# One more weight slot, shared row buffers and an earlier scatter in a two-layer mixture-of-experts trunk

## The chip, the cores and the metric

The kernel runs on one core of one Trainium2 chip. The metric is the device time of one launch in microseconds (us). Before the change it is 742.02 us, the median of three runs (740.44 to 742.1). The profiled execution, from which all rows below come, took 742.91 us; its span from the first to the last instruction is 740.9 us.

## The reference

256 tokens of 1024 features pass through two layers; everything is float32. Layer 1 is retention (four heads, chunks of 128) with a gated output, layer 2 is causal attention (eight heads; with 256 tokens there is a single block, so the selection of past blocks is empty). Each is followed by a mixture of experts:

```python
def hier_moe(x, w_rg, b_rg, w_re, b_re, w_gate, w_up, w_down):
    ...
    g_prob = softmax(t @ w_rg + b_rg)           # 4 groups, the best one
    e_logits = ...                              # 4 experts in it, the best two
    combine = group_w[:, :, None] * within[:, None, :]
    for g in range(G):
        hg = silu(t @ w_gate[g]) * (t @ w_up[g])
        y = y + (hg * combine[:, g, :, None]) @ w_down[g]
```

There are 16 experts per layer, each with a gate and an up matrix of 1024 x 512 and a down matrix of 512 x 1024. Each token uses two of them. All 16 experts' weights have to be read once per layer: 96 MB (in units of 1,048,576 bytes), beside 48 MB of dense weights in all. The layers end in a residual sum, the whole in a normalisation.

## The kernel before

**Weights as units in a ring.** All weights are cut beforehand into units of 1 MB (8 KB in each of 128 partitions). `Ring` holds a list of the units in the order of their use and a list of free slots in on-chip memory. `add` appends a unit; `issue` (L147) starts the transfer of the next unit as soon as a slot is free; `done` gives a slot back when the last matmul that reads it has been placed, and issues again. All these transfers stand in the queue of one engine, SyncE (SP), in the order of the list, each behind a wait for its slot. There are 20 slots that are always in the ring (19, and one that is free after retention), and in an expert stage some more: two or three `flex` buffers that the dense stages use otherwise, the buffer of `h` while its content stands in PSUM, and `N_EXTRA` slots of a pool `late` that is opened with the expert stage (none before the change). `ring.cap` lets an expert stage fetch at most `CAPX` = 2 units of what follows it.

**An expert layer** (`moe`, called twice). Its first part routes the tokens: logits, choice of the group and of two experts, and each token's place in its experts. Up to 64 tokens go to each expert. Two experts are worked on together as a pair `j` (0 to 7): their 2 x 64 token rows fill the 128 partitions of one buffer. The units of a pair are four of gate, four of up, four of down; each holds its part of both experts. `h`, the residual stream, is copied to PSUM (`total`, four banks) and to a table `rows` in memory off the chip. For the first pair the rows are gathered by matmuls; for all others GpSimd's indirect DMA fetches them (`pull`, L947) into `xn`.

**The loop over pairs** (L1226 on; TensorE's and ScalarE's instructions stand in the order of the program here, the other engines' are placed by the scheduler). For pair `j`:

1. `silu` of the gate product (L1204), the four up units by `grow(j, "u", ...)` (matmuls of `expand`, L982; one unit serves two of the eight steps `k`), then `gate` multiplies both (L1210).
2. `turn_in` (L953) transposes the rows `xn` of pair j+1 and evicts them to `xg`, half on VectorE (L940) and half on ScalarE (L944); `COLS` says which half goes where.
3. `turned` (L997) transposes the gated product of pair j; VectorE copies the first half of it to `hd` (L999), ScalarE the second (L1000).
4. `scatter` of the pair before, j-1 (L1029, L1030): eight matmuls that add its outputs to `total`; four for each half `n` of the features.
5. `slots(j + 2)` computes which tokens stand in pair j+2, and starts its `pull`.
6. `project` (L1010): the down projection with the four down units into two PSUM banks.
7. `parts` evicts these in two parts, `yh` on ScalarE (L1021) and `yl` on VectorE (L1022), into four buffers of 2 KB that serve this alone (tag `ys`).
8. `grow(j + 1, "g", ...)`: the gate units of the next pair.

In the last pair of a layer the scatter of the pair before stands between `turned` and `project` as well; then its own `parts` and `scatter` follow, and `finish` (the final normalisation) or `restore`. `more()` is a loop for experts with over 64 tokens; it does not run with these inputs.

The lines at which a pair's turning, scatter and projection follow one another are

```python
                    hd = turned(hh, work("hd").rearrange("p (k j) -> p k j", k=4))
                    if ahead:
                        scatter(*ahead)
                    if j + 2 < NP:
                        slots(j + 2, ps)
                    yp = project(both, hd, weight_of(j), done_of(j))
```

**Buffers that the change touches.** `flex(n, ...)` gives a buffer with a tag; a new tile under the same tag waits until the readers of the one before are done. `flex3` (8 KB) holds `xl`, the low part of the transposed stream in the dense stages, and then, in an expert stage, `held`: `xn` and `xg`, 4 KB each. `work` is a rotation of two buffers of 2 KB for `gl` (the silu output) and `hd`.

Of the kernel before, what the change touches and what calls it, by code (L numbers as in the profile page):

```python
# [37 lines left out]
COLS = 0, 1  # L38
# [157 lines left out]
def trunk(ctx, tc, x, x_t, dense_in, moe_in, gain_in, par_in, fin_in, rot_in, dec_in, con_in, out):  # L196
    nc = tc.nc
    V = nc.vector
    N_BASE, N_FLEX, N_EXTRA = 20, 2, 0
# [13 lines left out]

    def x_parts():
        return flex(2, [128, KD, T], F32R, "xh"), flex(3, [128, KD, T], F32R, "xl")
# [27 lines left out]
    def moe_units(layer):  # L243
        for j in range(NP):
            for n, name in enumerate("gud"):
                for u in range(4):
                    U["moe", layer, j, name, u] = ring.add(
                        moe_in[layer, j, 4 * n + u].rearrange("p (k n) -> p k n", k=2 if name == "d" else 4))
# [18 lines left out]
    ident_b = const.tile([128, 128], BF16, name="ident_b")  # L267
# [192 lines left out]
    def retention():  # L460
        with tc.tile_pool(name="ret_w", bufs=2, reuse_waits="tile") as wpool:
# [98 lines left out]
            for n, (a, b, unit, pieces) in enumerate(FIRST):  # L560
# [3 lines left out]
                if n == 0:  # L564
# [14 lines left out]
            nc.gpsimd.affine_select(out=ident_b, in_=ones_b, compare_op=OP.is_equal, fill=0.0, base=0,  # L579
                                    pattern=[[-1, 128]], channel_multiplier=1)  # L580
# [187 lines left out]
    def router(layer, junk):  # L768
# [3 lines left out]
        held = flex(3, [128, 2, D], F32, "held")  # L772
        xn = held[:, 0]
        xg = held[:, 1].rearrange("p (k j) -> p k j", k=KD)
# [28 lines left out]
    def moe(layer):  # L803
        g0 = G_FFN[layer]
        with tc.tile_pool(name="extra", bufs=1, side="right", reuse_waits="tile") as late, \
# [219 lines left out]
            def scatter(ys, st, end=False):  # L1025
                for n in range(2):
# [52 lines left out]
            def slots(j, bank=pt):  # L1079
                RS[j], idx = slot_values(sel_of(j), [cs[:, tt, j] for tt in range(NT)],  # L1080
                                         [con[:, C_SELC + 12 * n:C_SELC + 12 * n + 12] for n in range(2)], bank)
                if j:
                    pull(idx, xn)
# [128 lines left out]
            with tc.manual_schedule(engines={mybir.EngineType.PE}):  # L1212
# [9 lines left out]
                slots(1)  # L1222
                grow(0, "g", range(4, 8))
                ring.open([h.rearrange("p t d -> p (t d)")], moe_end[layer])
                ahead = None
            with tc.manual_schedule(engines={mybir.EngineType.PE, mybir.EngineType.Activation}):  # L1226
                for j in range(NP):
# [8 lines left out]
                    if j + 1 < NP:  # L1236
                        for n in range(2):
                            turn_in(xn, xg, range(4 * n, 4 * n + 4), COLS[n])
                    hd = turned(hh, work("hd").rearrange("p (k j) -> p k j", k=4))
                    if ahead:  # L1240
                        scatter(*ahead)
                    if j + 2 < NP:
                        slots(j + 2, ps)
                    yp = project(both, hd, weight_of(j), done_of(j))
                    st = transposed_select(rs, t1("ST", [128, T], F32R, bufs=2))
                    if j + 2 < NP:
                        ahead = parts(yp), st
                        grow(j + 1, "g", range(0, 8))
                    elif j + 1 < NP:
# [93 lines left out]
```

## Time and profile before

| | |
|---|---|
| median of three runs | 742.02 us (740.44 to 742.1) |
| profiled execution | 742.91 us, span 740.9 us |
| TensorE busy | 720.5 us (97%) |
| VectorE, ScalarE, GpSimd busy | 320.1, 270.4, 35.9 us |
| chain that ended last | TensorE 62%, DMA 34%, VectorE 2% |
| moved | 263.24 MB, 355 GB/s in the mean |
| granted clock of TensorE | 0.997 in the mean |

Times within the span are counted from its start. The stages are: retention up to about 204 us, routing and start of the first expert layer to about 217, its pairs to about 415, attention to about 521, routing again, and the pairs of the second expert layer and the end. A busy share is no measure of what limits a stage: a matmul counts as busy through its pipeline, so TensorE can look full while it waits a little for each unit. Rows of transfers give the issue on the sync queue; "landing" is when the data is reported as there.

### The profile page before, as it was taken

To read this page: it belongs to the slowest core of one execution; us is meant where nothing else is said; L and a number is where in the kernel's file an instruction comes from. 1 tells how busy PE (TensorE), PEld (TensorE's weight loads), DVE (VectorE), ACT (ScalarE), POOL (GpSimd) and SP (SyncE) were. 2 spreads that over 40 slices of the span, in tenths; PEclk is the share of its full clock that TensorE was granted. 3 is DMA by queue.
4 is the path that set the end of the run, shared out by engine and by line. 5 is a ranking of instruction groups with operands and counts; after the bars stand their busy time and mean duration, and the time that the engine had idled before them with its cause. 6 is when DMAs were issued, how large, how long until landed. Compare 5 with 4: busy or idle time off the path is not lost.

```text
span 740.9 us, 10093 instructions
## 1 busy us (share of the span) xinstructions
PE 720.5 (97%) x3652; PEld 430.1 (58%) x3652; DVE 320.1 (43%) x893; ACT 270.4 (36%) x550; POOL 35.9 (5%) x48
## 2 busy tenths in 40 slices
PE   8999999999999999999999999999999999999984
PEld 6988898887863434443343688888733344434431
DVE  4976688667661202211110677765721121112103
ACT  5667554667431111111110778674411111111112
POOL 0000000001000000000000003130010000000000
PEclk9999999999999999999999999999999999999998
DMA  8999646577879999999999799757899999999993
GB/s 246 421 420 420 228 145 243 207 278 274 323 283 388 422 419 419 419 423 419 419 421 404 315 422 421 290 211 303 318 397 421 420 421 418 423 419 421 420 410 122
DMA packets 43366, 263.24 MB, mean 355 GB/s; under 512 B 5695, under 2 KB 6975, under 8 KB 13616
## 3 DMA queue, kind: packets, MB, share of 16 engines
q1 hardware_dynamic: 40752, 256.85, 86.5%
q0 software_dynamic: 2560, 5.71, 2.1%
q8 instruction: 30, 0.49, 0.3%
q14 instruction: 24, 0.20, 0.1%
HBM read 263.12 MB, written 3.15 MB: 359 GB/s over the span
## 4 chain that ended last, share of the span: by engine, by line
PE 62%; DMA 34%; DVE 2%; issue 1%; SPq 0%; ACT 0%; DVEq 0%; POOLq 0%; ACTq 0%
DMA slot<-in_moe_dram 22%; PE ps L982 10%; PE acc L347 10%; PE acc L345 10%; PE acc L346 10%; DMA h<-in_moe_dram 8%; PE pt L1010 7%; DMA held<-rows,idx 2%; PE acc L383 2%; PE acc L381 2%; PE acc L382 2%; PE ps L794 1%; DMA slot<-in_dense_dram 1%; PE pt L953 1%; PE pt L884 1%; PE acc L1030 1%
## 5 line engine op out<-in xcount | busy, mean ns | idle before, releaser
L982 PE MATMUL ps<-slot,held 128*64 128x512 f32 x816 | 184.8, 594 | 2.0 <-DMA slot<-in_moe_dram 1.6
L982 PEld LDWEIGHTS ps<-slot,held 128*64 128x64 f32 x816 | 58.5, 137 | 116.7 <-issue 104.7
L341 DVE SCALAR_TENSOR_TENSOR wlo<-slot,gain,whi 128x512 fp32r<-128x512 f32 x144 | 107.0, 752 | 37.4 <-ACT whi L340 35.8
L340 ACT ACTIVATE whi<-slot,gain 128x512 fp32r<-128x512 f32 x144 | 102.9, 721 | 55.4 <-PE acc L346 37.0
L1210 DVE SCALAR_TENSOR_TENSOR gl<-ps,rs,gl 128x256 f32<-128x256 f32 x32 | 14.0, 480 | 194.5 <-PE ps L982 194.5
L1010 PE MATMUL pt<-slot,hd 128*64 128x512 f32 x416 | 96.2, 596 | 1.0 <-DVE idx L962 0.5
L345 PE MATMUL acc<-whi,xh 128*128 128x512 f32 x224 | 91.1, 407 | 0.6 <-ACT whi L340 0.6
L346 PE MATMUL acc<-whi,xl 128*128 128x512 f32 x224 | 87.6, 391 | 0.0
L347 PE MATMUL acc<-wlo,xh 128*128 128x512 f32 x224 | 87.5, 393 | 0.1
L1022 DVE TENSOR_TENSOR yl<-pt,yh 128x512 fp32r<-128x512 f32 x32 | 22.1, 691 | 99.9 <-ACT yh L1021 99.9
L1021 ACT ACTIVATE yh<-pt 128x512 fp32r<-128x512 f32 x32 | 19.1, 597 | 115.5 <-PE pt L1010 115.5
L1010 PEld LDWEIGHTS pt<-slot,hd 128*64 128x64 f32 x416 | 28.5, 137 | 53.1 <-issue 51.1
L944 ACT ACTIVATE held<-pt,gain 128x128 f32<-128x128 f32 x60 | 17.2, 368 | 102.5 <-PE pt L953 99.0
L1204 ACT ACTIVATE gl<-ps,rs 128x256 f32<-128x256 f32 x32 | 13.4, 470 | 106.3 <-PE ps L982 106.3
L347 PEld LDWEIGHTS acc<-wlo,xh 128*128 128x128 f32 x224 | 42.0, 188 | 10.0 <-DVE wlo L341 0.5
L345 PEld LDWEIGHTS acc<-whi,xh 128*128 128x128 f32 x224 | 42.2, 188 | 8.9 <-ACT whi L340 0.9
L346 PEld LDWEIGHTS acc<-whi,xl 128*128 128x128 f32 x224 | 42.2, 188 | 8.2
L338 DVE TENSOR_TENSOR wlo<-slot,whi 128x512 fp32r<-128x512 f32 x44 | 30.2, 689 | 21.0 <-ACT whi L337 18.2
L337 ACT ACTIVATE whi<-slot 128x512 fp32r<-128x512 f32 x44 | 27.8, 632 | 28.3 <-DVE wlo L338 16.3
L381 PE MATMUL acc<-xh,whi 128*128 128x256 f32 x128 | 35.9, 281 | 1.7 <-ACT whi L340 1.7
L383 PE MATMUL acc<-xh,wlo 128*128 128x256 f32 x128 | 36.2, 284 | 0.4 <-DVE wlo L341 0.3
L382 PE MATMUL acc<-xl,whi 128*128 128x256 f32 x128 | 35.6, 279 | 0.0
(226 smaller groups left out, 933.1 us busy)
## 6 DMA issues: line engine op xcount, KB each, us to landing
slot<-in_moe_dram SPq DMA_DIRECT2D x152, 1024.0 KB, 19.8
slot<-in_dense_dram SPq DMA_DIRECT2D x43, 1024.0 KB, 17.5
flex_slot<-in_moe_dram SPq DMA_DIRECT2D x22, 1024.0 KB, 19.8
slot_v<-in_moe_dram SPq DMA_DIRECT2D x8, 1024.0 KB, 19.6
h<-in_moe_dram SPq DMA_DIRECT2D x6, 1024.0 KB, 19.8
slot<-in_dense_dram SPq DMA_DIRECT2D x16, 256.0 KB, 6.4
rows<-h POOLq DMA_DIRECT2D x2, 1024.0 KB, 8.8
flex_slot<-in_moe_dram SPq DMA_DIRECT2D x4, 512.0 KB, 17.7
```

The costliest lines, as they stand in the source:

```text
L337: nc.scalar.activation(hi, w, AF.Copy)
L338: V.tensor_tensor(lo, w, hi.bitcast(F32), op=OP.subtract)
L340: nc.scalar.activation(hi, w, AF.Copy, scale=g)
L341: V.scalar_tensor_tensor(lo, w, g, hi.bitcast(F32), op0=OP.mult, op1=OP.subtract)
L345: nc.tensor.matmul(p, a, wh, start=start, stop=False)
L346: nc.tensor.matmul(p, l, wh, start=False, stop=False)
L347: nc.tensor.matmul(p, a, wl, start=False, stop=stop)
L381: nc.tensor.matmul(d, wh[:, s], xh[:, k], start=(k == 0 and c % 2 == 0), stop=False)
L382: nc.tensor.matmul(d, wh[:, s], xl[:, k], start=False, stop=False)
L383: nc.tensor.matmul(d, wl[:, s], xh[:, k], start=False, stop=(k == KD - 1 and c % 2 == 1))
L982: nc.tensor.matmul(p[s * w:(s + 1) * w], xg[:, k, s * w:(s + 1) * w], weight(name, k, s), start=(k == 0), stop=(k == KD - 1))
L1010: nc.tensor.matmul(yp[n][s * w:(s + 1) * w], hd[:, k, s * w:(s + 1) * w], weight("d", k, s)[:, n * 512:(n + 1) * 512], start=(k == 0), sto ...
```

## The change

It does the following:

- `N_EXTRA` is 1: an expert stage has one more slot of 8 KB per partition, in the pool `late`, open to the units of that stage only.
- The `ys` buffers are gone. The low half of the features (`n` = 0) of `yh` and `yl` goes to a tile `ylow` under the new tag `flex4`, 4 KB, the other half to the `work` rotation. `flex4` also holds `xn` (`rows_in`). `xl` is split into two tiles of 4 KB (`Halves`), in `flex3` and `flex4`; `xg` has `flex3` alone. `ST` has one buffer instead of two, and the unused `ident_b` is dropped.
- The order of the units: gate unit 0 of pair j+1 stands ahead of the four down units of pair j.
- In the loop the scatter of a pair follows its own projection, with gate step pair 0, 1 of the next pair between `turned` and `project` and steps 2, 3 between `parts` and `scatter`. The pull for pair j+2 follows the scatter, then gate steps 4 to 7. For pair 6 only the half `n` = 1 is scattered there; the half `n` = 0 follows the gating of pair 7, ahead of its `turned`.
- `COLS` swaps the engines of the two evictions in `turn_in`; the small product of `slots` goes to a `pt` bank instead of `ps`; `transposed_select` stands ahead of `project`.

```diff
-COLS = 0, 1
+COLS = 1, 0
...
-    N_BASE, N_FLEX, N_EXTRA = 20, 2, 0
+    N_BASE, N_FLEX, N_EXTRA = 20, 2, 1
...
     def x_parts():
-        return flex(2, [128, KD, T], F32R, "xh"), flex(3, [128, KD, T], F32R, "xl")
+        return flex(2, [128, KD, T], F32R, "xh"), Halves([flex(3 + n, [128, 4, T], F32R, f"xl{n}") for n in range(2)])
+
+    def rows_in():
+        return flex(4, [128, D], F32, "xn")
...
+            for n in range(3):
+                if n == 2 and j + 1 < NP:
+                    add(j + 1, 0, 0)
                 for u in range(4):
+                    if j == 0 or n + u:
+                        add(j, n, u)
...
             def parts(yp):
                 ys = []
+                low = flex(4, [128, 2, 512], F32R, "ylow")
                 for n in range(2):
-                    ys.append([t1(name, [128, 512], F32R, bufs=4, tag="ys") for name in ("yh", "yl")])
+                    ys.append([work(name, F32R) if n else low[:, i] for i, name in enumerate(("yh", "yl"))])
...
                     if j + 1 < NP:
                         for n in range(2):
                             turn_in(xn, xg, range(4 * n, 4 * n + 4), COLS[n])
+                    else:
+                        scatter(ys, st, ns=(0,))
                     hd = turned(hh, work("hd").rearrange("p (k j) -> p k j", k=4))
-                    if ahead:
-                        scatter(*ahead)
+                    if j + 1 < NP:
+                        grow(j + 1, "g", range(0, 2))
                     if j + 2 < NP:
-                        slots(j + 2, ps)
+                        idx = slots(j + 2)
+                    st = transposed_select(rs, t1("ST", [128, T], F32R))
                     yp = project(both, hd, weight_of(j), done_of(j))
-                    st = transposed_select(rs, t1("ST", [128, T], F32R, bufs=2))
-                    if j + 2 < NP:
-                        ahead = parts(yp), st
-                        grow(j + 1, "g", range(0, 8))
-                    elif j + 1 < NP:
-                        ahead = parts(yp), st
-                        grow(j + 1, "g", range(0, 4))
+                    if j + 1 < NP:
+                        ys = parts(yp)
+                        grow(j + 1, "g", range(2, 4))
+                        scatter(ys, st, ns=range(0 if j + 2 < NP else 1, 2))
+                        if j + 2 < NP:
+                            xn = rows_in()
+                            pull(idx, xn)
+                            grow(j + 1, "g", range(4, 8))
+                            continue
                         with tc.issue_after(ring.last.ins):
                             more()
```

## Rows read from the trace of the kernel before

**Rows 1.** The page's 40 equal slices of the span (18.5 us each): the GB/s that were moved.

```profile
GB/s 246 421 420 420 228 145 243 207 278 274 323 283 388 422 419 419 419 423 419 419 421 404 315 422 421 290 211 303 318 397 421 420 421 418 423 419 421 420 410 122
```

**Rows 2.** The table by stage: stretch in us, its length, busy us of PE, PEld, DVE, ACT and POOL with their instructions, granted clock, DMA share, GB/s.

```profile
255.00:398.00 143.00, 142.63 (x691) 56.17 (x689) 25.25 (x90) 20.88 (x55) 5.00 (x5) 1.00 1.01 420
415.00:521.00 106.00, 105.34 (x511) 87.59 (x512) 74.22 (x170) 73.51 (x155) 15.28 (x17) 1.00 0.84 336
...
636.00:717.00 81.00, 79.75 (x386) 30.81 (x384) 12.34 (x40) 12.87 (x32) 1.99 (x2) 1.00 1.02 420
```

**Rows 3.** The chain that ended last, its last transfer: start, length, what.

```profile
697.02 19.80 DMA slot<-in_moe_dram
```

**Rows 4.** TensorE in order of time over one pair of the second expert layer: `turn_in` of one pair, the first gate units behind its projection, `turn_in` of the next pair.

```profile
595.94 1.09 PE L953 MATMUL pt<-ident,held 128*128 128x128 f32 x8
...
606.25 1.89 PE L982 MATMUL ps<-flex_slot,held 128*64 128x512 f32 x8
...
620.09 1.09 PE L953 MATMUL pt<-ident,held 128*128 128x128 f32 x8
```

**Rows 5.** The same table as rows 2, microsecond by microsecond, at the start of the first and of the second expert layer; the last two columns are the DMA share and the GB/s.

```profile
213.00:214.00 1.00, 1.00 (x14) 1.00 (x11) 1.00 (x8) 0.00 (x0) 0.00 (x0) 1.00 0.83 311
214.00:215.00 1.00, 1.00 (x11) 0.88 (x12) 0.81 (x8) 0.63 (x2) 0.00 (x0) 1.00 0.14 57
215.00:216.00 1.00, 1.00 (x7) 0.42 (x8) 1.00 (x4) 0.00 (x0) 0.00 (x0) 1.00 0.08 33
216.00:217.00 1.00, 1.00 (x8) 0.29 (x4) 0.51 (x3) 0.00 (x0) 0.00 (x0) 1.00 1.06 205
...
533.00:534.00 1.00, 1.00 (x6) 0.29 (x4) 0.97 (x4) 0.00 (x0) 0.00 (x0) 1.00 0.86 360
534.00:535.00 1.00, 1.00 (x8) 0.39 (x6) 0.32 (x2) 0.00 (x0) 0.00 (x0) 1.00 0.90 221
535.00:536.00 1.00, 1.00 (x8) 0.19 (x4) 0.00 (x0) 0.00 (x0) 0.00 (x0) 1.00 0.63 221
```

**Rows 6.** The sync queue in order of time at the start of both expert layers.

```profile
204.61 0.33 SPq L147 DMA_DIRECT2D flex_slot<-in_moe_dram  x1
208.92 0.33 SPq L147 DMA_DIRECT2D slot<-in_moe_dram  x1
215.08 0.33 SPq L147 DMA_DIRECT2D h<-in_moe_dram  x1
...
527.07 0.78 SPq L147 DMA_DIRECT2D flex_slot<-in_moe_dram  x1
533.77 0.33 SPq L147 DMA_DIRECT2D h<-in_moe_dram  x1
```

**Rows 7.** In order of time, pair 0 of the first expert layer: the transposes of `turned`, the two copies to `hd`, the projection.

```profile
232.12 0.60 PE L997 MATMUL ps<-ident,gl 128*128 128x128 f32 x4
...
232.75 0.42 DVE L999 COPY hd<-ps 128x256 f32<-128x256 f32 x1 [0.18 <-PE ps L960]
...
233.23 3.22 PE L1010 MATMUL pt<-slot,hd 128*64 128x512 f32 x14 [0.48 <-DVE idx L962]
...
233.33 0.40 ACT L1000 ACTIVATE hd<-ps 128x256 f32<-128x256 f32 x1
```

**Rows 8.** In order of time, the last pair of each expert layer: in the second one the last up unit, gating, transposes, first scatter matmul, copy to `hd`, last scatter matmul, projection; of the first one the last up unit and the projection.

```profile
716.87 1.94 PE L982 MATMUL ps<-slot,held 128*64 128x512 f32 x8 [0.54 <-DMA slot<-in_moe_dram]
...
718.91 0.87 DVE L1210 SCALAR_TENSOR_TENSOR gl<-ps,rs,gl 128x256 f32<-128x256 f32 x2 [14.51 <-PE ps L982]
...
719.54 0.74 PE L997 MATMUL ps<-ident,gl 128*128 128x128 f32 x4 [0.73 <-DVE gl L1210]
...
720.03 0.49 PE L1029 MATMUL acc<-yh,ST 128*128 128x512 f32 x1
...
720.31 0.42 DVE L999 COPY hd<-ps 128x256 f32<-128x256 f32 x1 [0.53 <-PE ps L997]
...
721.74 0.40 PE L1030 MATMUL acc<-yl,ST 128*128 128x512 f32 x1
...
722.07 1.08 PE L1010 MATMUL pt<-slot,hd 128*64 128x512 f32 x4
...
398.41 1.94 PE L982 MATMUL ps<-slot,held 128*64 128x512 f32 x8 [0.54 <-DMA slot<-in_moe_dram]
...
403.59 1.08 PE L1010 MATMUL pt<-slot,hd 128*64 128x512 f32 x4
```

**Rows 9.** All gathers by GpSimd (L947): count, duration in ns (least, median, most), first and last start; time from issue to landing.

```profile
L947 POOL DMA_INDIRECT held<-rows,idx x14: 988/999/1136, 222.0 to 672.5; - x14
...
DMA to landing us min/median/max: 8.1/8.6/9.1
```

**Rows 10.** Two transfers of the last pair of the second layer, down unit 1 and the last piece of down unit 3: the issue, and the time from it to landing.

```profile
L147 SPq DMA_DIRECT2D flex_slot<-in_moe_dram x1: 328/328/328, 702.0 to 702.0; - x1
...
DMA to landing us min/median/max: 19.9/19.9/19.9
...
L147 SPq DMA_DIRECT2D slot<-in_moe_dram x1: 1819/1819/1819, 711.9 to 711.9; - x1
...
DMA to landing us min/median/max: 15.1/15.1/15.1
```

**Rows 11.** The page's list of transfers: out and in, queue, count, KB each, median us from issue to landing.

```profile
slot<-in_moe_dram SPq DMA_DIRECT2D x152, 1024.0 KB, 19.8
```

**Rows 12.** The table of rows 2 for the seven microseconds around the last up units.

```profile
713.00:720.00 7.00, 5.17 (x23) 1.34 (x20) 0.87 (x2) 0.00 (x0) 0.00 (x0) 1.00 1.00 406
```

More of the change, by code (lines that the diff above doesn't have):

```diff
@@ L212, in flex_slot, with __init__, __getitem__ @@
         return flex(n, [128, 2048], F32, f"flex_slot{n}")
+    class Halves:
+        def __init__(self, parts):
+            self.parts = parts
+        def __getitem__(self, at):
+            p, ks, *rest = at
+            if isinstance(ks, int):
+                return self.parts[ks // 4][(p, ks % 4, *rest)]
+            n = ks.start // 4
+            assert ks.stop <= 4 * n + 4
+            return self.parts[n][(p, slice(ks.start - 4 * n, ks.stop - 4 * n), *rest)]
     def x_parts():
-        return flex(2, [128, KD, T], F32R, "xh"), flex(3, [128, KD, T], F32R, "xl")
+        return flex(2, [128, KD, T], F32R, "xh"), Halves([flex(3 + n, [128, 4, T], F32R, f"xl{n}") for n in range(2)])
+    def rows_in():
+        return flex(4, [128, D], F32, "xn")
     def acc():
@@ L244, in moe_units, with add @@
         for j in range(NP):
-            for n, name in enumerate("gud"):
+            def add(j, n, u):
+                name = "gud"[n]
+                U["moe", layer, j, name, u] = ring.add(
+                    moe_in[layer, j, 4 * n + u].rearrange("p (k n) -> p k n", k=2 if name == "d" else 4))
+            for n in range(3):
+                if n == 2 and j + 1 < NP:
+                    add(j + 1, 0, 0)
                 for u in range(4):
-                    U["moe", layer, j, name, u] = ring.add(
-                        moe_in[layer, j, 4 * n + u].rearrange("p (k n) -> p k n", k=2 if name == "d" else 4))
+                    if j == 0 or n + u:
+                        add(j, n, u)
         for u in (2, 3):
@@ L1023, in parts, with scatter @@
                 return ys
-            def scatter(ys, st, end=False):
-                for n in range(2):
+            def scatter(ys, st, end=False, ns=range(2)):
+                for n in ns:
                     for tt in range(NT):
@@ L1081, in slots @@
                                          [con[:, C_SELC + 12 * n:C_SELC + 12 * n + 12] for n in range(2)], bank)
-                if j:
-                    pull(idx, xn)
+                return idx
             def weight_of(j):
@@ L1221, in moe @@
                 select(1, pos)
-                slots(1)
+                pull(slots(1), xn)
                 grow(0, "g", range(4, 8))
                 ring.open([h.rearrange("p t d -> p (t d)")], moe_end[layer])
-                ahead = None
             with tc.manual_schedule(engines={mybir.EngineType.PE, mybir.EngineType.Activation}):
```

8 lines of the change are left out of this document (2 added, 6 removed).

## The prediction

> **What bounds the kernel now.** I read the page's slices first: in the two expert stretches (the 14th to 22nd and the 30th to 39th slice) the moved bytes stand at 418 to 423 GB/s but for their first and last slices, while in the dense stretches they go up and down [rows 1]. The table by stage says the same: 255 to 398 us and 636 to 717 us run at 420 GB/s with a DMA share above 1.00, attention (415 to 521 us) at 336 GB/s with TensorE busy for 105.34 of 106 us [rows 2]. TensorE is also "busy" in the expert stretches, but the chain of waits settles who sets the end there: it runs back through weight transfers only, and the last one before the end is the 697.02 us issue that takes 19.80 us to land [rows 3]. A pair of experts is 12 units of 1 MB, 12 x 1.0486 MB / 420 GB/s = 30.0 us of transfer; TensorE needs 24.15 us for the same pair where nothing keeps it waiting (595.94 to 620.09 us) [rows 4]. So each expert layer ends at (sum of its bytes) / 420 GB/s, plus every microsecond in which the engines of the DMA stood still since the layer began, plus the tail behind the last up unit. Attention between them is bound by TensorE and passes a shift on whole.
>
> The stand-still is in the rows per microsecond: in layer 0 the rate falls to 311, 57, 33 and 205 GB/s from 213 to 217 us; in layer 1 to 360, 221 and 221 from 533 to 536 us [rows 5]. The sync queue shows why: it had no free slot. In layer 0 it issues at 204.61 and 208.92 us and then nothing until `h` comes free at 215.08; in layer 1 its last issue of the routing is at 527.07, and the next is `h` at 533.77 us [rows 6]. As shares of 420 GB/s the missing parts are 0.26 + 0.86 + 0.92 + 0.51 = 2.55 us and 0.14 + 0.47 + 0.47 = 1.08 us.
>
> **The change, part by part.** *One more unit slot.* It holds 1 MB, 2.50 us of transfer at 420 GB/s. It comes with the expert stage, beside flex slot 1, whose transfer goes out at 204.61 us [rows 6]; its bytes belonged to the dense stage's split weights, whose last reader is the same last dense matmul that frees that flex slot. So I expect its issue between 204.6 and 209.3 us, and 2.50 us more queued work: it fills the hole of 2.55 us in layer 0, gain 2.50. In layer 1 all that can be filled is the hole, 1.08 us: the rest of the megabyte only moves later what runs on without a stop (397 to 423 GB/s from there to the last slices [rows 1]). Bounds: 0 in both layers if the slot is released only after the hole; 2.50 in both if smaller dips later on vanish too. I take 2.5 + 1.1 = 3.6 us, since the holes are the rows nearest to it.
>
> *Order of units and gate steps.* Gate unit 0 of the next pair is fetched and used ahead of the four down units. It is the same 12 MB per pair, and behind the last up unit come the same four down units as before. TensorE's matmuls are the same too. Between the turning and the down projection the old kernel has eight scatter matmuls to cover the eviction of `hd`; now one gate unit, 13.84 us / 8 = 1.73 us [rows 4], covers it. Cost 0 while the transfers are behind; without that cover it would be at most the 0.42 us copy plus 0.40 us on ScalarE per pair [rows 7], and TensorE has 30.0 - 24.15 = 5.8 us to spare per pair. The swapped eviction order, one `ST` buffer instead of two, the small product of the slots in another PSUM bank, and `ident_b` (one GpSimd instruction at the start) lie under the same cover: 0.
>
> *The pull.* `xn` and the low halves of the outputs now share one buffer, so the gather for pair j+2 waits on TensorE's first half scatter of pair j. On GpSimd nothing is queued behind it but later gathers. With P as the end of the projection: one gate unit 1.73, four scatter matmuls 0.97 (the last of eight starts 1.71 after the first, 0.24 each [rows 8]), so it starts at P + 2.7 and lands after 8.1 to 9.1 us [rows 9], at P + 10.8 to P + 11.8. TensorE wants it after that gate unit, eight scatter matmuls, two gate units and four up units: P + 1.73 + 1.94 + 3.46 + 6.92 = P + 14.0. Spare 2.2 us in the stretch where TensorE leads, more where it waits for weights. Cost 0. The Trainium skill's page "DMA: Bandwidth & Descriptors", in "Anatomy of one DMA — SWDGE (gpsimd) path", prices such a transfer at about 2.0 us plus bytes over 436 GB/s, by which 128 rows of 4 KB would land in an estimated 3.2 us and the spare be some 8 us. The trace does not agree: 8.1 us is the shortest of 14 [rows 9], and the measured one is used.
>
> *The tail of each layer.* This is the second gain. In the last pair the up matmuls end at 716.87 + 1.94 = 718.81, the gating at 719.78, the four transposes at 720.28, the copy of `hd` at 720.73, and the projection begins only at 722.07, because the eight scatter matmuls of pair 6 stand between [rows 8]. After the change four of them are done in pair 6, where TensorE waits for weights anyway, and four stand ahead of the turning, from 718.83 to 719.80: beside the gating. The turning, 0.60 us in the first pair [rows 7], then ends at 720.40, the copy at 720.85, and the projection can begin at 720.91: in the first pair, which has no scatter, it began at 233.23, 0.06 after the copy and before ScalarE's half was done [rows 7]. That is 722.07 - 720.91 = 1.16 us earlier. The next limit is the down units: the second lands at 701.99 + 19.9 = 721.9 [rows 10], the projection (32 matmul records in 7.04 us) would want it after 4 of them, at 721.79: 0.11 us of wait; the last column piece lands at 711.92 + 15.1 = 727.0 [rows 10], wanted after 28, at 727.2. So 1.05 us. In layer 0 the last up unit starts at 398.41 and the projection at 403.59, the same 5.2 us as in layer 1 [rows 8], so the same 1.05. Bounds: 0, if the projection waits for both halves of `hd` and a late piece; 1.16.
>
> **The sum.** 2.5 + 1.1 + 1.05 + 1.05 = 5.7 us. The profiled execution took 742.91 us (span 740.9 and 2.0 around it): 737.2. It lies 0.89 above the median of the three timed runs, 742.02, so I forecast 742.02 - 5.7 = 736.3 us.
>
> **The rivals.**
> *The slot adds nothing* (its bytes are free only after 217 us, or the hole just moves to the next dip). Then only the tails are left: 742.0 - 2.1 = 739.9. For it: in layer 1 the hole is less than half a unit. Against: two other slots are in transfer by 209 us.
> *The tails add nothing* (the down units land too late): 742.0 - 3.6 = 738.4. For it: the 0.11 us of wait, and 0.2 of slack at the last piece.
> *More than forecast*: the whole 2.50 us in layer 1 as well, and 1.16 in each tail: 742.0 - 7.3 = 734.7.
> *The change doesn't reach the bound*: some later stretch takes back what was won, 742.
> *Slower: the late pull.* The place is the turning of `xn` in pairs 1 to 6. A loop closes: half scatter, pull of L us, turning of `xn` 1.09 [rows 4], transposes 0.60 [rows 7], a gate unit 1.73, projection 7.04, gate unit and half scatter 2.70, so a pair cannot be shorter than L + 13.2. It decides once that exceeds 30.0 us, from L = 16.8. If the pull stood in line like a weight unit, 19.8 us [rows 11], each of the 6 such pulls per layer would cost 3.0 us: 12 x 3.0 - 5.7 = +30, 772 us. Against: the gathers of this kernel took 8.1 to 9.1 us with that line standing [rows 9].
> *Slower: TensorE's clock falls in the tail*, where half of the scatter leaves a gap. Two projections of 7.1 us at 1.2 instead of 2.4 GHz: +14.2 - 5.7, 750.5. Against: from 713 to 720 us TensorE was busy for 5.17 of 7 us, waiting for units, and the granted clock stayed 1.00, the 2.4 GHz level [rows 12]; the new gap is under 1 us. The Trainium skill's page "TensorE: Matmul & The Clock Gate", section "HAM oscillation — how this bites in real kernels", says that waits for transfers between bursts of matmuls can throw the clock back each time. [...]
>
> **How the numbers follow.** Forecast 56%, more than forecast 6%, no gain in the tails 12%, no gain from the slot 14%, nothing 5%, late pull 4%, clock 3%. A change of 0.3%, 2.2 us, is about what a measurement tells from none. The slot rival's 739.9 lies just at that edge: 6 of its 14 I count as faster. Faster 56 + 6 + 12 + 6 = 80%, same 8 + 5 = 13%, slower 7%. The range goes from 734.2, just below "more than forecast", to 740.2, just above "no gain from the slot".
>
> **What would show it.** After: no microsecond under 300 GB/s from 213 to 217 us and from 533 to 536 us (shifted by the gain so far); one more weight issue in the sync queue ahead of `h`; the last up unit of layer 0 landing about 2.5 us earlier, that of layer 1 about 4.65 (2.5 + 1.05 + 1.1); from that landing to the first projection matmul about 4.1 us instead of 5.2; still 8 to 9 us for a pull and no long wait of the transposes for it. I am wrong if TensorE waits for `xn`, if the holes stay, or if the rate in the expert stretches falls below 420 GB/s.

## The result: slower, and the profile after

The changed kernel takes 745.61 us (median of five runs, 744.75 to 746.86) against 742.02 us (five runs, 740.44 to 742.9): a ratio of 1.0052, 95% interval 1.004 to 1.0064. It is 3.6 us slower; the forecast was 736.3 us, 5.7 us faster. The profiled execution took 746.86 us.

The page of the changed kernel: the engines' busy time, the moved GB/s in 40 slices, and of the groups the main one of `expand`, whose last column is the idle time of TensorE ahead of it and what ended it.

```profile
PE 728.4 (98%) x3652; PEld 431.1 (58%) x3652; DVE 322.5 (43%) x893; ACT 271.8 (36%) x550; POOL 35.2 (5%) x47
...
GB/s 240 421 420 421 206 158 237 216 261 272 328 318 412 422 420 420 420 420 418 421 420 398 332 421 388 234 199 312 334 388 422 420 419 421 419 421 420 419 406 95
...
L1000 PE MATMUL ps<-slot,xg 128*64 128x512 f32 x824 | 190.3, 596 | 0.3
```

The same group on the page of the kernel before:

```profile
L982 PE MATMUL ps<-slot,held 128*64 128x512 f32 x816 | 184.8, 594 | 2.0 <-DMA slot<-in_moe_dram 1.6
```

This row says what [rows 1] and [rows 3] hide. The transfers run at 420 GB/s in both kernels; but in the kernel before, TensorE waited for them for 1.6 us in this group over the whole run (2.5 us by the starts of its matmuls, below), and now no longer at all. TensorE's busy time rose by 7.9 us, from 720.5 to 728.4, with the same 3652 matmul records. The bound is TensorE, and it has more time to fill.

Where it fills it is seen in one pair of the second layer, TensorE in order of time. After the change:

```profile
601.07 1.09 PE L971 MATMUL pt<-ident,xn 128*128 128x128 f32 x8
602.00 0.64 PE L1015 MATMUL ps<-ident,gl 128*128 128x128 f32 x4
602.57 1.94 PE L1000 MATMUL ps<-slot,xg 128*64 128x512 f32 x8
604.44 0.21 PE L978 MATMUL pt<-cs,S 128*128 128x13 bf16 x2
604.58 7.09 PE L1028 MATMUL pt<-slot,hd 128*64 128x512 f32 x32
611.49 1.89 PE L1000 MATMUL ps<-flex_slot,xg 128*64 128x512 f32 x8
613.31 0.50 PE L1048 MATMUL acc<-ylow,ST 128*128 128x512 f32 x1
...
615.36 3.65 PE L1000 MATMUL ps<-slot,xg 128*64 128x512 f32 x16
...
625.82 1.09 PE L971 MATMUL pt<-ident,xn 128*128 128x128 f32 x8
```

The kernel before, the part of its pair that [rows 4] leaves out:

```profile
596.88 0.64 PE L997 MATMUL ps<-ident,gl 128*128 128x128 f32 x4
597.27 0.47 PE L1029 MATMUL acc<-yh,ST 128*128 128x512 f32 x1
...
599.20 0.21 PE L960 MATMUL ps<-cs,S 128*128 128x13 bf16 x2
599.34 7.09 PE L1010 MATMUL pt<-slot,hd 128*64 128x512 f32 x32
...
607.97 5.32 PE L982 MATMUL ps<-slot,held 128*64 128x512 f32 x24
```

From start to start, since the modelled lengths overlap:

| step | before | after |
|---|---|---|
| turning of `xn` (8) | 0.94 | 0.93 |
| `turned` (4) | 0.39 | 0.57 |
| scatter (8) | 1.93 | 2.05 |
| slots (2) | 0.14 | 0.14 |
| projection (32) | 6.91 | 6.91 |
| gate and up (64) | 13.84 | 1.87 + 1.82 + 10.46 = 14.15 |
| pair | 24.15 | 24.75 |

No matmul was added, and no row of the pair shows a wait. Each step lengthens where the kind of its neighbour changed. `expand` and `project` keep 64 columns of the stationary operand at a time ("128\*64"), the transposes, slots and scatter 128. Before, a pair had two changes of kind (into the projection, out of the up units); now it has six. The 0.60 us more are the same in pairs 1 to 5 of both layers. (Pair 0 now does a scatter of its own, pair 6 has half a scatter and no slots, so these two compare otherwise.)

The tail did what was forecast. The last pair of the second layer after the change, TensorE:

```profile
721.95 1.92 PE L1000 MATMUL ps<-slot,xg 128*64 128x512 f32 x8
723.79 0.50 PE L1048 MATMUL acc<-ylow,ST 128*128 128x512 f32 x1
...
725.94 2.37 PE L1028 MATMUL pt<-slot,hd 128*64 128x512 f32 x10 [0.52 <-DVE hd L1017]
```

From the start of the last up unit to the projection it was 722.07 - 716.87 = 5.20 us before [rows 8]; it is 725.94 - 721.95 = 3.99 now: 1.2 us gained per layer (5.18 and 4.00 in layer 0), forecast 1.05 with 1.16 as the bound. And the last unit is used without a wait.

The slot filled the hole of layer 0; in layer 1 the hole only moved. The sync queue after the change at the start of both layers:

```profile
211.02 0.99 SPq L147 DMA_DIRECT2D extra<-in_moe_dram  x1
216.80 0.33 SPq L147 DMA_DIRECT2D h<-in_moe_dram  x1
...
530.95 1.20 SPq L147 DMA_DIRECT2D extra<-in_moe_dram  x1
537.71 8.01 SPq L147 DMA_DIRECT2D slot<-in_moe_dram  x4
545.89 1.11 SPq L147 DMA_DIRECT2D h<-in_moe_dram  x1
```

Single microseconds of the changed kernel (columns as in rows 2):

```profile
215.00:216.00 1.00, 1.00 (x11) 1.00 (x10) 1.00 (x10) 0.13 (x1) 0.00 (x0) 1.00 1.05 434
216.00:217.00 1.00, 1.00 (x9) 0.73 (x9) 0.81 (x7) 0.50 (x2) 0.00 (x0) 1.00 0.99 410
...
539.00:540.00 1.00, 1.00 (x6) 0.31 (x4) 0.44 (x6) 0.00 (x0) 0.00 (x0) 1.00 0.71 270
```

Where 33 and 205 GB/s stood [rows 5] there are 434 and 410. In layer 1 the rate is now 418 to 442 from 534 to 539 us, but 270 and 279 from 539 to 541. The unit in `h` there stands behind four others: 545.89, not 533.77 [rows 6]. Without the slot (x1_noslot below) it goes out at 534.01, ahead of them.

The wait for units before, in the last pair of each layer:

```profile
393.94 3.93 PE L982 MATMUL ps<-flex_slot,held 128*64 128x512 f32 x16
...
711.90 1.94 PE L982 MATMUL ps<-slot,held 128*64 128x512 f32 x8
714.39 1.94 PE L982 MATMUL ps<-slot,held 128*64 128x512 f32 x8 [0.55 <-DMA slot<-in_moe_dram]
```

A unit takes 1.72 us among its own kind (606.25 to 607.97). In layer 0 two units took 398.41 - 393.94 = 4.47, so 1.0 us of wait; in layer 1 two took 716.87 - 711.90 = 4.97, so 1.5.

From start to start, layer 0 and layer 1 then change in these steps. Pair 0: +2.0 and +1.9, since it does its own scatter now. Pairs 1 to 5: 5 x 0.60 = +3.0 each. From the turning of pair 6 to the last up unit: -1.8 and -2.5, since the wait is gone and half a scatter less stands there. The tail: -1.2 each. That is +2.0 and +1.2, 3.2 us of the 3.9 by which the two profiled executions differ; the rest lies outside the layers. The medians differ by 3.6.

### The profile page after: what moved, and what is told of

It is laid out like the page before. It is cut to its first block, busy times and chain, and to the rows that moved or that the text cites. A ratio compares the mean times of both kernels' runs of the same rounds, so it can differ in the third digit from the quotient of the medians.

```text
span 744.8 us, 10065 instructions
## 1 busy us (share of the span) xinstructions
PE 728.4 (98%) x3652; PEld 431.1 (58%) x3652; DVE 322.5 (43%) x893; ACT 271.8 (36%) x550; POOL 35.2 (5%) x47
## 5 line engine op out<-in xcount | busy, mean ns | idle before, releaser
L1000 PE MATMUL ps<-slot,xg 128*64 128x512 f32 x824 | 190.3, 596 | 0.3
L1000 PEld LDWEIGHTS ps<-slot,xg 128*64 128x64 f32 x824 | 57.7, 137 | 106.4 <-issue 95.8
L1028 PE MATMUL pt<-slot,hd 128*64 128x512 f32 x384 | 86.9, 595 | 0.5 <-DVE hd L1017 0.5
L1028 PEld LDWEIGHTS pt<-slot,hd 128*64 128x64 f32 x384 | 26.5, 137 | 49.0 <-issue 46.2
L962 ACT ACTIVATE xg<-pt,gain 128x128 f32<-128x128 f32 x60 | 17.2, 367 | 94.7 <-PE pt L971 91.2
L1041 DVE TENSOR_TENSOR ylow<-pt,ylow 128x512 fp32r<-128x512 f32 x16 | 11.1, 692 | 87.5 <-ACT ylow L1040 87.5
L1040 ACT ACTIVATE ylow<-pt 128x512 fp32r<-128x512 f32 x16 | 9.6, 597 | 98.5 <-PE pt L1028 98.5
L359 DVE TENSOR_TENSOR wlo<-slot,whi 128x512 fp32r<-128x512 f32 x48 | 32.9, 690 | 23.5 <-ACT whi L358 20.7
L358 ACT ACTIVATE whi<-slot 128x512 fp32r<-128x512 f32 x48 | 30.3, 631 | 31.3 <-DVE wlo L359 15.9
## 6 DMA issues: line engine op xcount, KB each, us to landing
slot<-in_moe_dram SPq DMA_DIRECT2D x147, 1024.0 KB, 19.8
flex_slot<-in_moe_dram SPq DMA_DIRECT2D x21, 1024.0 KB, 19.8
```

The costliest lines, as they stand in the source:

```text
L358: nc.scalar.activation(hi, w, AF.Copy)
L359: V.tensor_tensor(lo, w, hi.bitcast(F32), op=OP.subtract)
L1000: nc.tensor.matmul(p[s * w:(s + 1) * w], xg[:, k, s * w:(s + 1) * w], weight(name, k, s), start=(k == 0), stop=(k == KD - 1))
L1028: nc.tensor.matmul(yp[n][s * w:(s + 1) * w], hd[:, k, s * w:(s + 1) * w], weight("d", k, s)[:, n * 512:(n + 1) * 512], start=(k == 0), sto ...
```

## The experiments

Theory A: TensorE is the bound but for the last pair, and each pair of changes between the two kinds of matmul costs it about 0.3 us. Theory B: the transfers are the bound, as predicted, or waits for evictions are what lengthens the pair. "Layers" below is the time from the turning of pair 0 to the projection of pair 7, both layers added, against the kernel before (172.4 + 173.0 us); it comes from one profiled execution each, where the medians come from several.

| run | pair, us | layers | median, us | ratio to before, 95% |
|---|---|---|---|---|
| changed kernel | 24.74 | +3.2 | 745.61 | 1.004 to 1.0064 |
| x1_noslot | 24.74 | +3.3 | 745.08 | 1.0033 to 1.0066 |
| x2_slots_first | 24.80 | +4.5 | 745.83 | 1.0041 to 1.0072 |
| x3_split_scatter | 24.51 | +1.7 | 745.01 | 1.003 to 1.0065 |
| x4_halves | 24.15 | -0.7 | 742.17 | 0.9988 to 1.0016 |
| x6_slots_ps | 25.67 | +14.4 | 756.18 | 1.0176 to 1.0225 |
| x7_after_noscatter | 22.54 | -5.5 | 737.16 | 0.992 to 0.9971 |
| x8_before_noscatter | 22.83 | -3.8 | 739.06 | 0.9957 to 0.9989 |
| x9_slots_at_scatter | 24.49 | +0.9 | 742.23 | 0.9991 to 1.0018 |
| x10_before_tail | 24.14 | -2.6 | 739.28 | 0.9945 to 0.9974 |
| x12_h_after_gather | 24.49 | +0.2 | 741.89 | 0.9991 to 1.0014 |
| x13_before_slots_in_gate | 24.39 | +0.3 | 742.65 | 1.0002 to 1.0027 |

The kernel before had medians of 741.2 to 741.9 us beside these runs.

**The slot taken out of the changed kernel.**

```diff
-    N_BASE, N_FLEX, N_EXTRA = 20, 2, 1
+    N_BASE, N_FLEX, N_EXTRA = 20, 2, 0
```

> The change without its slot (N_EXTRA = 0). Theory A: after the change TensorE alone sets the end of both expert layers, because its pair grew from 24.14 to 24.74 us through more changes between matmuls with 64 and with 128 stationary columns; the transfers run ahead, so the slot is worth nothing now: 745 to 746.5 us, pair 24.74 us. Theory B, that of my forecast: the transfers set the end and the slot is worth 3.6 us: about 749 us. Theory C: the change is slower because the slot shifts other transfers: about 742 us.

745.08 us, pairs of 24.74 us, and no wait for units in the last pair without the slot either. The megabyte is worth nothing to the changed kernel: TensorE came too late to need it. No run has the slot with the old order of steps, so what it is worth there isn't measured.

**The buffers alone.** The kernel before with `xl` in two tiles, `xn` under `flex4` and `ident_b` dropped.

```diff
-        return flex(2, [128, KD, T], F32R, "xh"), flex(3, [128, KD, T], F32R, "xl")
+        return flex(2, [128, KD, T], F32R, "xh"), Halves([flex(3 + n, [128, 4, T], F32R, f"xl{n}") for n in range(2)])
...
```

> The kernel before with the split of xl into two tiles, xn in the second of them, and without ident_b; loop, units and slots untouched. In the one profile of the change, retention ended 1.72 us later than before (logits at 206.50 against 204.78 us). If that is the split's doing: logits near 206.5 and 743.7 us. If it is the start of that one execution (1.3 us of it are there 30 us after the start): logits within 0.6 us of 204.8, and 742 us.

742.17 us: the split costs nothing. (The sharing of `ylow` with `xn`, and the single `ST`, are not in this run.) Its profile has layers 0.7 us shorter than those of the kernel before at the same median, so single profiles differ by that much.

**Half of the scatter moved, in the kernel before.** The second half stands behind the projection in pairs 1 to 6; `scatter` takes the halves as a list `ns`.

```diff
-                    if ahead:
-                        scatter(*ahead)
+                    old = ahead
+                    if old:
+                        scatter(*old, ns=(0,) if j + 1 < NP else range(2))
...
+                    if old and j + 1 < NP:
+                        scatter(*old, ns=(1,))
```

> The kernel before, with the second half of the scatter of the pair before moved behind the down projection (pairs 1 to 6): two more changes of matmul shape per pair, nothing else. Theory A: pair 24.14 to 24.35-24.45 us; the last pair's wait for up units (2.24 us in the first layer, 2.89 in the second) shrinks by six times that, to about 0.7 and 1.4 us, and the time stays within 0.7 us of 742. Theory D: pair stays 24.14 us, waits as before.

TensorE of this run around the moved half:

```profile
606.00 0.50 PE L1029 MATMUL acc<-yh,ST 128*128 128x512 f32 x1
...
607.13 1.94 PE L982 MATMUL ps<-flex_slot,held 128*64 128x512 f32 x8
```

One more pair of changes, 24.51 us per pair: +0.36. The moved four matmuls take 607.13 - 606.00 = 1.13 us, where the eight in a row took 1.93. The wait in the last pair is gone. Six pairs of each layer are changed: 12 x 0.36 = 4.3 less 2.5 of wait gives +1.8, and the layers of the profiled execution show +1.7. The median shows +3.3 (interval +2.2 to +4.8); the profiled execution, 743.57, was the fastest of four. So the order alone, with no slot and no shared buffer, makes the kernel before slower; I had put the time within 0.7 us of 742, since I thought that the transfers would hide more of it.

**The slots ahead of the gate unit, in the changed kernel.**

```diff
-COLS = 1, 0
+COLS = 0, 1
...
-                    if j + 1 < NP:
-                        grow(j + 1, "g", range(0, 2))
                     if j + 2 < NP:
                         idx = slots(j + 2)
+                    if j + 1 < NP:
+                        grow(j + 1, "g", range(0, 2))
```

> The change, with the small slots product moved ahead of the first gate unit, next to the transposes, and the eviction order put back (COLS = 0, 1). That takes away two of the four added changes of matmul shape per pair. Theory A: pair 24.74 to about 24.43 us, 7 pairs per layer, so some 2 us per layer less until the transfers bind again: 741 to 742.5 us. Theory D (TensorE waits on the shared buffers, the pull or the evictions, not on the change of shape): pair still 24.7 us and 745 to 746.5 us.

The shape gain came, and a wait ate it: the slots now take a bank of `pt` while VectorE evicts it. TensorE of this run:

```profile
625.81 0.64 PE L1015 MATMUL ps<-ident,gl 128*128 128x128 f32 x4
626.61 0.19 PE L978 MATMUL pt<-cs,S 128*128 128x13 bf16 x2 [0.16 <-DVE xg L958]
626.73 1.94 PE L1000 MATMUL ps<-slot,xg 128*64 128x512 f32 x8
628.50 1.03 PE L1028 MATMUL pt<-slot,hd 128*64 128x512 f32 x4
```

The `turned` step grew from 0.57 to 0.80, the gate unit shrank from 1.87 to 1.77. The pair could not tell the theories apart.

**The slots ahead of `turned`, in a bank of `ps`.**

```diff
+                    if j + 2 < NP:
+                        idx = slots(j + 2, ps)
                     hd = turned(hh, work("hd").rearrange("p (k j) -> p k j", k=4))
...
-                    if j + 2 < NP:
-                        idx = slots(j + 2)
```

> The changed kernel with the two small matmuls of the slots moved from behind the inserted gate unit to ahead of the turning, into the PSUM bank that the kernel before gave them; the order of the column halves stays as changed, so that they find no bank in eviction. Theory A (TensorE is the bound, and each change between the 64-column matmuls of expand and project and the 128-column ones costs it about 0.15 us): the gate unit then runs into the projection with no change of shape between, two changes per pair are gone, a pair takes 24.40 to 24.45 us instead of 24.74, each expert layer is 2 to 2.3 us shorter than after the change, or as much shorter as the transfers then allow, and the whole about 741 us (740 to 742.5). Rival B (the 0.60 us per pair come from a wait on the eviction of hd or of the turned xn, not from changes of shape): the pair stays at 24.7 us and the time at 745 to 746 us.

756.18 us, a miss of both theories. `ps` has two banks; `turned` takes the second, and the gate unit needs the first back from the four small VectorE operations on the slots, which stand behind the eviction of `xn`. What TensorE waited for in this run (us in total, times, longest):

```profile
PE ps L1000 <- DVE rs_tmp L985: 7.8, 9, 0.9
PE ps L1000 <- DVE rs L987: 1.7, 2, 0.9
```

With a twelfth wait of 0.9 us, which the view puts down to a transfer, that is 0.9 us in each of the twelve pairs that have slots, and nothing hides it: a pair takes 0.93 more than in the changed kernel, 12 x 0.93 = 11.2 us, and the layers show +14.4 in place of +3.2. The median is 15.0 above the kernel before. This is the plainest sign that TensorE bounds the layer: a wait of 0.9 us, far less than the 5.8 us "to spare per pair", came through whole.

**The slots beside the scatter.** The same two matmuls moved to the one place where both neighbours allow it: behind matmuls that must end anyway, ahead of their own kind, in a bank that the scatter waits for as well.

```diff
-                    if j + 2 < NP:
-                        idx = slots(j + 2)
...
                         grow(j + 1, "g", range(2, 4))
+                        if j + 2 < NP:
+                            idx = slots(j + 2)
                         scatter(ys, st, ns=range(0 if j + 2 < NP else 1, 2))
```

> The changed kernel with the two small matmuls of the slots moved from between the inserted gate unit and the projection to the place right ahead of the scatter of the same pair, in the same PSUM bank family. There they stand beside matmuls of their own shape, and the bank that they take is the one whose eviction the scatter awaits anyway, so no new wait is to come. Theory A (each pair of changes between the 64-column and the 128-column matmuls costs TensorE about 0.3 us): one pair of changes goes, a pair of experts takes 24.40 to 24.45 us instead of 24.74, each layer gives back about 2.1 us, and the whole takes 741 to 742.5 us. Rival (the 0.60 us are the eviction of hd and xg as such): the pair stays within 0.1 us of 24.74 and the time at 745 to 746 us.

TensorE of this run:

```profile
606.55 1.89 PE L1000 MATMUL ps<-flex_slot,xg 128*64 128x512 f32 x8
608.37 0.21 PE L978 MATMUL pt<-cs,S 128*128 128x13 bf16 x2
608.43 0.47 PE L1048 MATMUL acc<-ylow,ST 128*128 128x512 f32 x1
...
622.41 1.94 PE L1000 MATMUL ps<-slot,xg 128*64 128x512 f32 x8
624.17 1.03 PE L1028 MATMUL pt<-slot,hd 128*64 128x512 f32 x4
```

Pair 24.49, time 742.23: 3.4 us of the 3.6 came back by moving two matmuls that take 0.14 us. They now take 0.06 (608.37 to 608.43), and the gate unit ahead of the projection 1.76 in place of 1.87. In the profile the layers are 2.4 us shorter than in the changed kernel: 12 x 0.25 = 3.0, less 0.6 us of wait for a unit that is back in the last pair of layer 1.

**The control: a pair of changes added to the kernel before.**

```diff
-                    if j + 2 < NP:
-                        slots(j + 2, ps)
...
-                        grow(j + 1, "g", range(0, 8))
+                        grow(j + 1, "g", range(0, 2))
+                        slots(j + 2)
+                        grow(j + 1, "g", range(2, 8))
```

> The kernel before with nothing moved but the two 13-column matmuls of the slots: from between scatter and projection into the gate steps of the next pair, behind the first unit. No work is added, one pair of changes from 64-column to 128-column matmuls and back is. Theory A: the pair of experts takes 24.35 to 24.5 us instead of 24.15 in pairs 0 to 5, although the moved matmuls themselves take 0.14 us; part of the 1.2 to 2 us per layer disappears in the last pair's wait for units. Time 741.5 to 744. Rival (only waits cost, changes of shape are free): 24.15 within 0.05 us, 741 to 742.

TensorE of this run around the moved matmuls:

```profile
606.14 1.89 PE L982 MATMUL ps<-flex_slot,held 128*64 128x512 f32 x8
607.96 0.21 PE L960 MATMUL pt<-cs,S 128*128 128x13 bf16 x2
608.10 5.37 PE L982 MATMUL ps<-slot,held 128*64 128x512 f32 x24
```

No work and no wait added, and the pair takes 24.39, +0.24: a gate unit 1.82 in place of 1.72, the scatter 2.02 in place of 1.93. Here the last pair's wait of 1.0 and 1.5 us, which is gone, pays for most of it: 12 x 0.24 = 2.9 less 2.5, +0.4; the layers show +0.3, the medians +0.9. With +0.36 (x3) and -0.25 (x9), a pair of changes is worth 0.24 to 0.36 us.

**What the transfers alone allow.** Both kernels without the scatter of pairs 0 to 6, so that their outputs lack these products. The kernel before:

```diff
-                    if ahead:
-                        scatter(*ahead)
```

The changed kernel:

```diff
-                    else:
-                        scatter(ys, st, ns=(0,))
...
-                        scatter(ys, st, ns=range(0 if j + 2 < NP else 1, 2))
```

> The kernel before with the scatter matmuls of pairs 0 to 6 left out in both expert layers (the output lacks their products). If TensorE is the bound of the kernel before but for its last pair, a pair goes at 22.0 to 22.3 us as long as units are on chip, the wait for units begins some pairs earlier than the last, and the layer ends no more than 2 to 3 us earlier than with the scatter, since the stream of transfers sets the end at once: 737 to 740 us in all. If the transfers were the bound all along, as the prediction had it, the time falls only by what stands behind the last unit, about 1 us per layer: 740 to 741 us.

> The changed kernel with the scatter matmuls of pairs 0 to 6 left out in both expert layers (their products are not added into the sum, so the output lacks them). This takes about 2 us per pair from TensorE. If the reading of the changed kernel is right, TensorE is the bound by a small margin only: the pair first goes at 22.1 to 22.7 us until the units on chip are used up, then the transfers set the pace, and each layer ends with the last unit's landing. Read against the kernel before with the same omission: one more slot is then worth 2.5 to 3.5 us in layer 0 and about nothing in layer 1, where the transfer into h is issued late. Rival (the slot is worth nothing to the transfers either): both layers equal to those of the kernel before with the same omission within 0.7 us.

Now TensorE waits. The group of `expand` on the page of the kernel before without scatter:

```profile
L982 PE MATMUL ps<-slot,held 128*64 128x512 f32 x816 | 186.4, 595 | 8.0 <-DMA slot<-in_moe_dram 7.9
```

and of the changed kernel without scatter:

```profile
L1000 PE MATMUL ps<-slot,xg 128*64 128x512 f32 x824 | 190.5, 596 | 7.6 <-DMA slot<-in_moe_dram 7.5
```

Before: 739.06 us, 2.1 less, though a pair now takes 22.83 us, 1.3 less. (The scatter had taken 1.93; without its cover the projection waits about 0.5 us for `hd` in each pair.) The layers are 1.5 and 2.3 us shorter in the profile, and 1.25 and 1.27 of that are the tail, where no scatter stands any more. Counted from the turning of pair 0, the last up unit is used only 0.2 and 1.1 us earlier: so close behind TensorE stand the transfers. With the slot, layer 0 is another 2.0 us shorter (168.9 against 170.9 us) and layer 1 not at all (171.0 against 170.7): the slot's worth was nearly as I had it in layer 0, but only for a TensorE that is there in time.

**`h` opened earlier, on top of the slots beside the scatter.**

> As the run with the slots at the scatter, and besides the buffer h is opened for weights ahead of the first gate steps of pair 0, where the changed kernel opens it behind the last, so that its transfer stands ahead of the others in the sync queue in both layers. If TensorE is the bound of that kernel in both layers, the time is the same within 0.7 us. If the transfers still set the end of layer 1 (the last up unit waited for), h's transfer goes out at about 12 us after the routing's end instead of 20, and layer 1 gains up to 1.1 us.

That try took 765.33 us and says nothing on its question: the opening stood ahead of pair 0's gather, which then read weights in place of the stream in `h` and waited up to 10.6 us for them. The next one put it behind the gather:

```diff
                 gather(1, 1)
+                ring.open([h.rearrange("p t d -> p (t d)")], moe_end[layer])
                 grow(0, "g", range(0, 2))
...
-                ring.open([h.rearrange("p t d -> p (t d)")], moe_end[layer])
```

> As the run with the slots at the scatter, and besides h is opened for weights right behind the matmuls of pair 0's gather, its last readers, and ahead of the first gate steps (the run with h opened early had put it ahead of those readers, which then waited for the weights; that run says nothing on this question). If h's transfer then leaves ahead of the first freed slots in layer 1, its last up units come up to 1.1 us earlier, and the wait of 0.67 us that is left in the last pair of layer 1 (11.12 us for the 48 steps against 10.45) goes: 0.6 to 0.7 us in all, about 741.5. Layer 0 stays within 0.3 us. Rival: h leaves as late as before (about 20 us after the routing's end) and nothing moves.

The sync queue of this run in layer 1:

```profile
532.50 0.33 SPq L147 DMA_DIRECT2D h<-in_moe_dram  x1
534.27 10.57 SPq L147 DMA_DIRECT2D slot<-in_moe_dram  x6
```

`h` leaves ahead of the freed slots again, and no microsecond from 531 to 566 us is under 410 GB/s: every hole of layer 1 is filled. The last wait for a unit is gone, and layer 1 is 0.6 us shorter than with the slots beside the scatter alone (172.8 against 173.4): that is all that the filled holes are worth to this TensorE. The median, 741.89, cannot show so little.

**The tail alone, on the kernel before.** In pair 6 one half of the scatter of that pair runs behind the first gate steps, in pair 7 the other ahead of `turned`.

```diff
+                    else:
+                        scatter(*ahead, ns=(1,))
                     hd = turned(hh, work("hd").rearrange("p (k j) -> p k j", k=4))
-                    if ahead:
+                    if ahead and j + 1 < NP:
                         scatter(*ahead)
...
                         grow(j + 1, "g", range(0, 4))
+                        scatter(*ahead, ns=(0,))
```

> The kernel before with one thing of the change alone, its tail: of pair 6's scatter one half runs behind the first four gate steps of pair 7 and the other ahead of the turning of pair 7; all other pairs as before, no extra slot. The change showed 1.09 us less between the last up matmul and the projection. The one pair of changes of shape that this adds per layer (about 0.35 us) falls in front of the last pair, where TensorE waits 2.2 to 2.9 us for units. If the tail term stands alone, each layer is 1.0 to 1.1 us shorter and the whole takes 738.9 to 739.9 us. Rival (the wait for the down units takes its place): 741 us, as before.

739.28 us, 2.6 less than before (1.9 to 4.1) and 6.3 less than the changed kernel's median. TensorE in the last pair of layer 1:

```profile
704.79 0.50 PE L1029 MATMUL acc<-yh,ST 128*128 128x512 f32 x1
...
716.77 0.50 PE L1029 MATMUL acc<-yh,ST 128*128 128x512 f32 x1
...
718.92 1.08 PE L1010 MATMUL pt<-slot,hd 128*64 128x512 f32 x4 [0.52 <-DVE hd L999]
```

2.15 us from the first scatter matmul behind the up matmuls to the projection (716.77 to 718.92), as in the changed kernel (723.79 to 725.94). The half scatter at 704.79 and its pair of changes fall in front of units that TensorE waited for anyway. It is the one part of the change that a run here shows to pay, and it needs neither the slot nor the shared buffers.

## Why the prediction was wrong

**The step that failed** is "Cost 0 while the transfers are behind", with its reserve, "TensorE has 30.0 - 24.15 = 5.8 us to spare per pair". Both numbers are right, the conclusion is not. TensorE needs 24.15 us for a pair whose transfers take 30.0; but it begins a layer with the ring full of units. One row of the kernel before shows the stock, the first use of the unit that was issued into `h` at 533.77 us [rows 6]:

```profile
587.26 1.89 PE L982 MATMUL ps<-h,held 128*64 128x512 f32 x8
```

That is 53 us behind its issue, where a transfer takes 19.8 us even with the queue full [rows 11] and this one took at most 8.3. TensorE eats 5.8 us of this stock per pair and does not wait for a unit until the last pair. A steady pair of 24.15 us in the middle of the layer [rows 4], not of 30.0, was the evidence, and I had quoted it as a sign of reserve.

**What bounds the kernel now** failed before it, in the reading of [rows 3]. The chain followed back the last unit, which was late by 0.5 us, and then walked through transfers that stand one behind another whoever waits for them; I took its length for a bound. Whether the queue sets the pace is told by the consumer's idle time, 1.6 us in the group of `expand`, and there I had not looked. The bounds lie within some microseconds: a layer cannot gain more than its wait, 1.0 or 1.5 us, from any amount of faster transfer of weights, as long as TensorE stays as it is. None of the signs that I had named for being wrong told of it: the rate stayed at 420 GB/s, the holes closed where they had been, and TensorE waited for `xn` once, for 0.3 us.

**The slot**, +2.5 and +1.1, follows the same error. The issue came at the very end of the forecast stretch (211.02; this execution runs 1.7 us later, flex slot 1 at 206.33) and the hole of layer 0 is filled; by the wait before, at most 1.0 us of it could have been felt, and the slower pair had used that up. In layer 1 the term would have failed by itself: the freed slots that the extra unit let through took the place of `h` in the queue, and the hole moved, as the slot rival had it. The reading that the transfers run on there without a stop was wrong too: it went by the mean of a slice, and in the kernel before the slice of 397 [rows 1] hides two microseconds of 184 and 266 GB/s, from 543 to 545 us.

**The order of units and gate steps**, costed at nothing: +0.60 us in each of pairs 1 to 5, 6.0 us in both layers. I had counted instructions and covers, and no row of one pair in one order shows what another order costs. The rival "the change doesn't reach the bound" came nearest, at 742, with 5%; none of the rivals was TensorE becoming slower at equal work and full clock.

**What was right**: the tail (1.2 us per layer against 1.05, a little over the bound of 1.16); the pull, which took 7.8 to 8.7 us to land and kept TensorE waiting once, for 0.3 us; the split of `xl` at nothing (x4_halves), and the shared buffers as far as no wait for them stands in the rows; TensorE's clock, granted at 1.00 from 720 to 735 us.

## What to carry to other kernels

Ask of a saturated queue whether anybody waits for it: the idle time of the consumer, group by group, decides, and the chain of waits does not where a stock of landed data lies between. Work out both bounds for the whole layer with its starting stock, not for one period; where they meet at the end, a gain on one side is cut off at the distance to the other. On TensorE count the seams between kinds of matmul beside the matmuls themselves, and put small matmuls of one kind next to others of that kind, in a bank that nobody is evicting.

## What the runs showed of the hardware

TensorE takes longer where matmuls with 64 columns of the stationary operand and such with 128 columns follow one another: eight `expand` matmuls take 1.72 us among their own, 1.82 us ahead of the scatter or the slots, 1.87 behind `turned` and ahead of the slots; the two slots matmuls take 0.06 us ahead of the scatter and 0.14 ahead of 64-column ones. One change there and back is 0.24 to 0.36 us, and in no row does it stand as idle time. A change of step within one kind costs nothing: in the kernel before, the last four projection matmuls ahead of a gate unit take 0.85 us (629.54 to 630.39), the four before them 0.86. What inside the engine takes the time wasn't tried and stays open; nor do the runs separate the number of columns from the other thing that sets the 64-column matmuls apart, that they write the two halves of a bank's partitions by turns.
